# Two pairs of experts share one end, and the down weights are laid out by blocks of columns

## The chip, the cores and the metric

The kernel runs on one core of a Trainium2 chip. The metric is the device time of one execution in microseconds (us): the median of three runs of the kernel before.

## What is computed

A network of two layers works on 256 context tokens and 256 latent tokens of 1024 channels, in float32. Layer 0 has a gated linear-attention mixer (HGRN2) and then a mixture of experts over all 512 tokens; layer 1 has a latent-attention mixer (MLA) and then a mixture of experts over the 256 latent tokens, which are the output. The mixture of experts is the part that matters here. Each token goes to two of 32 experts, and an expert is

```python
def expert_block(args):
    xb, e = args
    return (jax.nn.silu(xb @ w_gate[e]) * (xb @ w_up[e])) @ w_down[e]
...
return jnp.einsum('nkd,nk->nd', y_slot.reshape(n_tok, MOE_TOP_K, d), gate_w.astype(h.dtype))
```

with `w_gate` and `w_up` of 1024 x 512 and `w_down` of 512 x 1024. The weighted sum is multiplied by a gate vector for each channel (`rG` in the kernel) and added to the residual `x`.

## The kernel before

**Pairs.** The 32 experts of a layer are worked through as 16 pairs, i = 0 to 15, in the function `stream`. Each expert has 64 slots for tokens, and a pair fills the 128 rows of the TensorE array: slots of the one expert in the left half, slots of the other in the right half, so every product of a pair is two half-wide matmuls, one for each expert's weights.

**One pair**, in the order of the program: load gate weights (two slots of 2 MB, one for each expert), `product` (L1038, 16 matmuls of 512 columns), Silu on ScalarE (L1173); load up weights, `product`; `hidden` (L1048, VectorE: Silu times up); `turn_hidden` (four transposes on TensorE, L1055, and a copy on ScalarE, L1057); `onehot` (L1062, VectorE: the matrix G that sends slots back to tokens); load down weights; `down` (L1069, two halves of 512 output columns, 16 matmuls each). Then `weighed` makes of each half two tiles yH and yL that carry the weighted result in two parts (ScalarE L1075, then VectorE L1076), and `give_back` runs once for each tile of 128 tokens (four in layer 0, two in layer 1): two matmuls with G (L1086 with yH, L1087 with yL) into one PSUM bank, a VectorE multiply by `rG` into `tmp` (L1089), and an add to `x` (L1090).

**Buffers.** yH, yL and G have one buffer each, so the next yL is written only after the last matmul that reads the one before it.

**Overlap between pairs.** `back` is a generator: the give-backs of pair i are issued in two halves during pair i+1, the first after its gate product and the second after its up product (the two `next(bk, None)`).

**The last pair** (i = 15) has nothing after it. `finish` cuts its down product into four blocks of 256 columns; block n+1 is multiplied before block n is given back. In these give-backs the odd token tiles use other PSUM banks, and the adds of the odd tiles of the first three blocks run on GpSimd (`adder=G`): six in layer 0, three in layer 1. In layer 1 each finished block is written out.

**What sets the order.** In `stream` TensorE, VectorE and ScalarE keep the order of the program (a manual schedule). All weight loads are issued by SyncE's one queue, in program order, into seven slots of 2 MB in layer 0 and nine in layer 1 that go round in a fixed list; a load waits until the slot's last reader is done. After layer 0's stream, `mla_load` loads the mixer's first weights and makes eight small matmuls (L1249), a branch on "more tokens than slots" follows (not taken with these inputs), and the mixer of layer 1 starts on all engines behind that branch.

Of the kernel before, what the change touches and what calls it, by code (L numbers as in the profile page):

```python
# [32 lines left out]
def prepare(inputs):  # L33
# [41 lines left out]
    o["rw"] = rw.reshape(2, 8, 128, 36).transpose(0, 2, 1, 3)  # L75
    o["wg"] = a["moe_w_gate"].reshape(2, 32, 128, 4096)
    o["wu"] = a["moe_w_up"].reshape(2, 32, 128, 4096)
    o["wd"] = a["moe_w_down"].reshape(2, 32, 128, 4096)
    return {k: np.ascontiguousarray(v) for k, v in o.items()}


# [1 line left out]
class K:  # L83
# [819 lines left out]
    def moe(self):  # L903
# [5 lines left out]
        with self.moe_st, ExitStack() as st:  # L909
# [108 lines left out]
                        give(xT, pt, b)  # L1018
                return xT

            def wload(src, i, parts=1, by=1, one=False):

                ws = [self.slot() for _ in range(2)]
                turns = [(c, a) for c in range(parts) for a in range(2)]
                for c, a in sorted(turns, key=lambda t: t[1]) if one else turns:
                    e = 2 * i + a
                    s_ = src[l, e] if isinstance(i, int) else src[l, bass.ds(e, 1)].rearrange("o p f -> (o p) f")
                    if parts == 1:
                        nc.sync.dma_start(ws[a], s_)
                    else:  # L1030
                        w_, s_ = [t.rearrange("p (j n c) -> p j n c", j=by, n=parts)[:, :, c, :] for t in (ws[a], s_)]
                        nc.sync.dma_start(w_, s_)
                return ws

            def product(p, xT, ws, k):
# [11 lines left out]
            def hidden(hi, p_up):  # L1047
                V.tensor_tensor(hi, hi, p_up, op=ALU.mult)  # L1048

            def turn_hidden(hi):  # L1050

                pt = self.sm()
                hv = hi.rearrange("p (q j) -> p j q", j=4)
                for j in range(4):
                    PE.transpose(pt[:, j * 128:(j + 1) * 128], hv[:, j, :], self.ident)  # L1055
                hT = hidT()
                S.copy(hT, pt.rearrange("p (j t) -> p j t", j=4))  # L1057
                return hT

# [4 lines left out]

            def down(hT, ws, n, w_):
                p = self.mm()[:, 0:w_]
                for j in range(4):
                    for a in range(2):
                        PE.matmul(p[a * 64:(a + 1) * 64, :], hT[:, j, a * 64:(a + 1) * 64],  # L1069
                                  ws[a][:, j * 1024 + n * w_:j * 1024 + n * w_ + w_], start=(j == 0), stop=(j == 3))  # L1070
                return p

            def weighed(p, wc, yH, yL):
# [4 lines left out]
            def parts():  # L1078
                return [b2.tile([128, 512], F32R, tag=t, name=t, bufs=1) for t in ("yH", "yL")]

            def give_back(tt, n, w_, Gm, yH, yL, bank=None, adder=V):

                ns = slice(n * w_, n * w_ + w_)
                pc = (bank or self.ac)()[:, 0:w_]
                g = Gm[:, tt * 128:(tt + 1) * 128]
                PE.matmul(pc, g, yH, start=True, stop=False)  # L1086
                PE.matmul(pc, g, yL, start=False, stop=True)  # L1087
                t = self.tmp()[:, 0:w_]
                V.tensor_tensor(t, pc, rG[vec(tt)][:, ns], op=ALU.mult)  # L1089
                adder.tensor_tensor(x[:, tt, ns], x[:, tt, ns], t, op=ALU.add)  # L1090

            def finish(hT, Gm, ws, wc, last):

                w_ = 256 if last else 512

                def scatter(n, yH, yL):
                    for tt in range(NT):
                        odd = last and tt % 2
                        give_back(tt, n, w_, Gm, yH, yL, self.sm if odd else None, G if odd and n < 3 else V)
                    if last and l:  # L1100
                        write_out_part(n, w_)

                yHL, todo = [], []
                for n in range(1024 // w_):
                    p = down(hT, ws, n, w_)
                    if n * w_ % 512 == 0:
                        yHL = parts()
                    yH, yL = [t[:, n * w_ % 512:n * w_ % 512 + w_] for t in yHL]
                    weighed(p, wc, yH, yL)
                    if todo:  # L1110
                        scatter(*todo.pop())
                    todo.append((n, yH, yL))
                scatter(*todo.pop())

            def pair(i, xT, fc, wc):

                pgu = []
                for src in (I["wg"], I["wu"]):
                    ws = wload(src, i)
                    p = self.mm()  # L1120
                    for k in range(8):
                        product(p, xT, ws, k)
                    pgu.append(p)
                ws = wload(I["wd"], i)
                hi = hid()
# [3 lines left out]
                finish(hT, onehot(fc), ws, wc, False)  # L1129

# [24 lines left out]
                return xT, step  # L1155

            def stream(p0, xT0):
                bk, xq, nxt, fstep = iter(()), xT0, None, None
                for i in range(16):
                    a, q = i % 2, i // 2  # L1160
                    if i and a == 0:
                        xq = nxt
                    xT = xq[a]
                    one, last = 2 if i == 1 else i == 2, i == 15
                    if i:
                        ws = wload(I["wg"], i, 4 if one else 2 if last else 1, one=one == 2 and l == 0)
                        p = self.mm()
                        for k in range(8):
                            product(p, xT, ws, k)
                    else:  # L1170
# [3 lines left out]
                    next(bk, None)  # L1174
# [10 lines left out]
                    next(bk, None)  # L1185
                    hT = turn_hidden(hi)
                    if q < 7:
                        fstep()
                    Gm = onehot(idxf[:, i:i + 1])
                    ws = wload(I["wd"], i, 4 if last or one else 1, 4 if last else 1)  # L1190
                    if last:
                        finish(hT, Gm, ws, wsl[:, i:i + 1], True)
                    else:
                        bk = back(i, [down(hT, ws, n, 512) for n in range(2)], Gm)
                        next(bk)

            def overflow():

# [334 lines left out]
```

## Time and profile before

| | |
|---|---|
| median of three runs | 1577.06 us (1576.94, 1577.06, 1578.92) |
| profiled execution | 1578.04 us |
| its span, first to last instruction | 1576.3 us |
| mean granted TensorE clock | 0.985 of full |
| TensorE busy | 1499.6 us (95%) |
| VectorE busy | 813.2 us (52%) |
| ScalarE / GpSimd busy | 449.1 / 74.9 us |
| moved by DMA | 500.80 MB, mean 318 GB/s |

The profiled execution lies 1.74 us above its own span, and 0.98 us above the median. The stream of layer 0 runs to about 919 us, the mixer of layer 1 follows, and the stream of layer 1 ends the kernel. A busy share is an average over stages with different limits, so the stages are read one by one below.

### The profile page before, as it was taken

The numbers are of one execution on the slowest core, as the hardware profiler recorded it, in microseconds if no ns is written. First come the engines' busy times: TensorE is split into PE (matmuls) and PEld (weight loads), VectorE is DVE, ScalarE is ACT, GpSimd is POOL, SyncE is SP. The second block draws the span as 40 slices with busy tenths as digits, with TensorE's granted clock in tenths as the row PEclk, the third lists the DMA queues.
The fourth block names the chain that finished last, engine by engine and source line by source line (L and its number), as shares of the span: only waits on it lengthen the run. The fifth ranks groups of instructions, "written<-read, shape, count | busy, mean of one in ns | idle before, by whom it ended". The sixth has DMA issues, their size and how long they took to land. (4 is left out here: it accounts for less than half of the span.)

```text
span 1576.3 us, 20139 instructions
## 1 busy us (share of the span) xinstructions
PE 1499.6 (95%) x8009; PEld 825.2 (52%) x8010; DVE 813.2 (52%) x1675; ACT 449.1 (28%) x938; POOL 74.9 (5%) x101
## 2 busy tenths in 40 slices
PE   7999999999899999999999999989799999998997
PEld 4777787778644544544544454447444443433433
DVE  5776647775824544544544567674534332332333
ACT  4554445553411111111111145554411111111110
POOL 0000000001300000000000011310100000000000
PEclk9999999999799999999999999999899999999999
DMA  9454534414769999999999957344799999999997
GB/s 384 165 201 177 196 136 161 188 54 161 276 240 399 429 428 426 428 427 426 427 429 423 356 218 305 141 187 142 272 392 428 427 427 428 428 427 428 427 425 268
DMA packets 63127, 500.80 MB, mean 318 GB/s; under 512 B 7024, under 2 KB 16624, under 8 KB 32816
## 3 DMA queue, kind: packets, MB, share of 16 engines
q1 hardware_dynamic: 59296, 490.87, 76.5%
q10 hardware_dynamic: 2816, 7.26, 1.4%
q0 software_dynamic: 912, 1.27, 0.3%
q8 instruction: 67, 1.10, 0.3%
q14 instruction: 36, 0.29, 0.0%
HBM read 498.26 MB, written 1.11 MB: 317 GB/s over the span
## 5 line engine op out<-in xcount | busy, mean ns | idle before, releaser
L1038 PE MATMUL mm<-w,xT 128*64 128x512 f32 x2048 | 469.9, 595 | 19.8 <-DMA w<-in_wg_dram 16.4
L1038 PEld LDWEIGHTS mm<-w,xT 128*64 128x64 f32 x2048 | 146.8, 137 | 310.7 <-issue 266.3
L1089 DVE TENSOR_TENSOR tmp<-p,rG 128x512 f32<-128x512 f32 (+1 forms) x106 | 68.0, 644 | 132.7 <-PE p L1087 132.6
L1090 DVE TENSOR_TENSOR x<-x,tmp 128x512 f32<-128x512 f32 (+1 forms) x195 | 132.4, 679 | 6.7
L1089 DVE TENSOR_TENSOR tmp<-p,x 128x512 f32<-128x512 f32 (+1 forms) x68 | 44.4, 655 | 165.1 <-PE p L1087 165.1
L1069 PE MATMUL mm<-w,x 128*64 128x512 f32 (+1 forms) x544 | 116.3, 570 | 1.6 <-ACT x L1057 1.4
L1069 PE MATMUL mm<-w,hT 128*64 128x512 f32 (+1 forms) x544 | 113.9, 570 | 1.4 <-ACT hT L1057 1.4
L889 PE MATMUL p<-sel,h2H 128*128 128x256 f32 x384 | 101.8, 300 | 1.8 <-DVE sel L879 1.8
L513 PE MATMUL mm<-hH,wH 128*128 128x512 f32 x256 | 101.9, 398 | 0.3 <-ACT wH L262 0.3
L515 PE MATMUL mm<-hH,wL 128*128 128x512 f32 x256 | 101.3, 396 | 0.5 <-DVE wL L264 0.5
L514 PE MATMUL mm<-hL,wH 128*128 128x512 f32 x256 | 100.6, 393 | 0.0
L890 PE MATMUL p<-sel,h2L 128*128 128x256 f32 x384 | 98.5, 290 | 0.0
L1076 DVE SCALAR_TENSOR_TENSOR yL<-mm,wsl,yH 128x512 fp32r<-128x512 f32 (+1 forms) x68 | 48.7, 716 | 71.6 <-ACT yH L1075 71.6
L1075 ACT ACTIVATE yH<-mm,wsl 128x512 fp32r<-128x512 f32 (+1 forms) x68 | 45.1, 663 | 123.3 <-PE mm L1069 93.2
L889 PEld LDWEIGHTS p<-sel,h2H 128*128 128x128 f32 x384 | 76.7, 200 | 5.1 <-issue 2.4
L264 DVE TENSOR_TENSOR wL<-w,wH 128x1024 fp32r<-128x1024 f32 x55 | 67.0, 1221 | 23.5 <-ACT wH L262 22.0
L1086 PE MATMUL p<-yH,G 128*128 128x512 f32 (+1 forms) x174 | 76.2, 441 | 0.9 <-DVE tmp L1089 0.9
L890 PEld LDWEIGHTS p<-sel,h2L 128*128 128x128 f32 x384 | 76.3, 199 | 1.4 <-issue 0.8
L1069 PEld LDWEIGHTS mm<-w,x 128*64 128x64 f32 x544 | 45.6, 137 | 60.0 <-issue 45.6
L262 ACT CAST wH<-w 128x1024 fp32r<-128x1024 f32 x55 | 57.3, 1047 | 63.3 <-PE mm L514 32.8
L1069 PEld LDWEIGHTS mm<-w,hT 128*64 128x64 f32 x544 | 37.5, 137 | 65.8 <-issue 59.7
L1086 PEld LDWEIGHTS p<-yH,G 128*128 128x128 f32 x174 | 32.5, 187 | 65.8 <-issue 51.5
(392 smaller groups left out, 2119.2 us busy)
## 6 DMA issues: line engine op xcount, KB each, us to landing
w<-in_wg_dram SPq DMA_DIRECT2D x52, 2048.0 KB, 18.1
w<-in_wu_dram SPq DMA_DIRECT2D x52, 2048.0 KB, 21.4
w<-in_wd_dram SPq DMA_DIRECT2D x52, 2048.0 KB, 20.2
aw<-in_ada_w_dram SPq DMA_DIRECT2D x32, 1024.0 KB, 6.0
w<-in_wd_dram SPq DMA_DIRECT2D x48, 512.0 KB, 8.7
w<-in_hg_w_dram SPq DMA_DIRECT2D x8, 2048.0 KB, 7.9
w<-in_wg_dram SPq DMA_DIRECT2D x32, 512.0 KB, 7.8
w<-in_wu_dram SPq DMA_DIRECT2D x32, 512.0 KB, 9.5
```

What stands on the lines that cost most here:

```text
L262: nc.scalar.copy(H, raw)
L264: nc.vector.tensor_tensor(L, raw, H, op=ALU.subtract)
L513: PE.matmul(p, H[:, c], hH[:, k, :], start=(k == 0), stop=False)
L514: PE.matmul(p, H[:, c], hL[:, k, :], start=False, stop=False)
L515: PE.matmul(p, L[:, c], hH[:, k, :], start=False, stop=(k == 7))
L889: self.nc.tensor.matmul(o, self.h2H[:, tt, c], r, start=(tt == 0 and k == 0), stop=False)
L890: self.nc.tensor.matmul(o, self.h2L[:, tt, c], r, start=False, stop=(last and k == 1))
L1038: PE.matmul(p[a * 64:(a + 1) * 64, :], xT[:, k, a * 64:(a + 1) * 64], ws[a][:, k * 512:(k + 1) * 512], start=(k == 0), stop=(k == 7))
L1069: PE.matmul(p[a * 64:(a + 1) * 64, :], hT[:, j, a * 64:(a + 1) * 64], ws[a][:, j * 1024 + n * w_:j * 1024 + n * w_ + w_], start=(j == 0), ...
L1086: PE.matmul(pc, g, yH, start=True, stop=False)
L1089: V.tensor_tensor(t, pc, rG[vec(tt)][:, ns], op=ALU.mult)
L1090: adder.tensor_tensor(x[:, tt, ns], x[:, tt, ns], t, op=ALU.add)
```

## The change

The host now lays the down weights of an expert out in four blocks of 256 output columns; within a block the four chunks of the contraction follow each other. A load of one block is 4 KB in a row in each partition, where it was four runs of 1 KB. `down` with 512 columns reads its moving operand as two runs of 256 columns, 1024 elements apart. This holds for every pair.

In each layer the last two pairs, 14 and 15, share one end. Pair 14's down product is no longer made before pair 15's gate product: gate and up of both pairs come first, then the down blocks of 14 and of 15, each block multiplied before the one ahead of it is given back. Layer 1 has eight blocks of 256 columns; layer 0 has two of 512 for pair 14 and four of 256 for pair 15. The give-backs of pair 14 therefore no longer run under pair 15's gate and up. The GpSimd adds are gone (all adds on VectorE), and odd token tiles always use the other banks in `finish`. Pair 15's gate and up weights are loaded ahead of pair 14's down weights.

```diff
-    o["wd"] = a["moe_w_down"].reshape(2, 32, 128, 4096)
+    wd = a["moe_w_down"].reshape(2, 32, 128, 4, 4, 256)
+    o["wd"] = wd.transpose(0, 1, 2, 4, 3, 5).reshape(2, 32, 128, 4096)
...
-                    if parts == 1:
-                        nc.sync.dma_start(ws[a], s_)
-                    else:
-                        w_, s_ = [t.rearrange("p (j n c) -> p j n c", j=by, n=parts)[:, :, c, :] for t in (ws[a], s_)]
-                        nc.sync.dma_start(w_, s_)
+                    f = slice(c * 4096 // parts, (c + 1) * 4096 // parts)
+                    nc.sync.dma_start(ws[a][:, f], s_[:, f])
...
             def down(hT, ws, n, w_):
                 p = self.mm()[:, 0:w_]
+                m = w_ // 256
                 for j in range(4):
                     for a in range(2):
-                        PE.matmul(p[a * 64:(a + 1) * 64, :], hT[:, j, a * 64:(a + 1) * 64],
-                                  ws[a][:, j * 1024 + n * w_:j * 1024 + n * w_ + w_], start=(j == 0), stop=(j == 3))
+                        w = ws[a].rearrange("p (n j c) -> p j n c", n=4, j=4)[:, j, n * m:(n + 1) * m, :]
+                        PE.matmul(p[a * 64:(a + 1) * 64, :].rearrange("p (n c) -> p n c", n=m), hT[:, j, a * 64:(a + 1) * 64], w,
+                                  start=(j == 0), stop=(j == 3))
...
-                adder.tensor_tensor(x[:, tt, ns], x[:, tt, ns], t, op=ALU.add)
...
+                V.tensor_tensor(x[:, tt, ns], x[:, tt, ns], t, op=ALU.add)
+
+            def finish(*todo, last=False):
+
+                yHL, wait = [], []
+
+                def scatter(n, w_, Gm, yH, yL, out):
                     for tt in range(NT):
-                        odd = last and tt % 2
-                        give_back(tt, n, w_, Gm, yH, yL, self.sm if odd else None, G if odd and n < 3 else V)
-                    if last and l:
+                        give_back(tt, n, w_, Gm, yH, yL, self.sm if tt % 2 else None)
+                    if out:
                         write_out_part(n, w_)
...
+                for z, (hT, i, fc, ws, w_) in enumerate(todo):
+                    for n in range(1024 // w_):
+                        p = down(hT, ws, n, w_)
+                        if n * w_ % 512 == 0:
+                            yHL = parts()
+                        yH, yL = [t[:, n * w_ % 512:n * w_ % 512 + w_] for t in yHL]
+                        weighed(p, i, yH, yL)
+                        if wait:
+                            scatter(*wait.pop())
+                        if n == 0:
+                            Gm = onehot(fc)
+                        wait.append((n, w_, Gm, yH, yL, last and l and z == len(todo) - 1))
+                scatter(*wait.pop())
...
-                    Gm = onehot(idxf[:, i:i + 1])
-                    ws = wload(I["wd"], i, 4 if last or one else 1, 4 if last else 1)
-                    if last:
-                        finish(hT, Gm, ws, wsl[:, i:i + 1], True)
-                    else:
+                    if i < 14:
+                        Gm = onehot(idxf[:, i:i + 1])
+                        ws = wload(I["wd"], i, 4 if one else 1)
                         bk = back(i, [down(hT, ws, n, 512) for n in range(2)], Gm)
                         next(bk)
+                    else:
+                        ends.append((hT, i))
+                todo = []
+                for hT, i in ends:
+                    w_ = 512 if l == 0 and i == 14 else 256
+                    todo.append((hT, wsl[:, i:i + 1], idxf[:, i:i + 1], wload(I["wd"], i, 1024 // w_), w_))
+                finish(*todo, last=True)
```

**TensorE at the end of layer 0, behind pair 14's transposes.** The numbers behind p and w are those of PSUM banks and weight slots. Before, its down matmuls (L1069) come next:

```order
L1086 MATMUL p_6437<-yH,G 128x512
L1087 MATMUL p_6437<-yL,G 128x512
L1055 MATMUL p_6443<-ident,tmp 128x128 x4
L1069 MATMUL mm<-w_3936,hT 64x512
L1069 MATMUL mm<-w_3937,hT 64x512
```

In the change pair 15's gate matmuls (L1036 there, L1038 before) stand at that place:

```order
L1086 MATMUL p_6437<-yH,G 128x512
L1087 MATMUL p_6437<-yL,G 128x512
L1053 MATMUL p_6443<-ident,tmp 128x128 x4
L1036 MATMUL mm<-w_3936,xT 64x512
L1036 MATMUL mm<-w_3937,xT 64x512
```

Pair 14's down product has moved behind gate and up of pair 15.

**VectorE at the end of layer 0.** Before, the first half of pair 14 is given back ahead of pair 15's `hidden` (L1048); these are the last of its rows, with the second half's first behind it:

```order
L1089 TENSOR_TENSOR tmp<-p_6517,rG_3389 128x512
L1090 TENSOR_TENSOR x<-x,tmp 128x512
L1076 SCALAR_TENSOR_TENSOR yL<-mm,wsl,yH 128x512
L1048 TENSOR_TENSOR tmp<-tmp,mm 128x512
L1089 TENSOR_TENSOR tmp<-p_6549,rG_3387 128x512
L1090 TENSOR_TENSOR x<-x,tmp 128x512
```

In the change `hidden` of pair 15 (L1046 there) comes ahead of all of them, and the two yL and the one G of pair 14 follow:

```order
L1046 TENSOR_TENSOR tmp<-tmp,mm 128x512
L1252 MEMSET w_3356 128x256
L1253 COPY w_3356<-colB_87 128x8x2
L1076 SCALAR_TENSOR_TENSOR yL<-mm,wsl,yH 128x512
L1060 TENSOR_SCALAR G<-iota,idxf 128x512
L1076 SCALAR_TENSOR_TENSOR yL<-mm,wsl,yH 128x512
L1089 TENSOR_TENSOR tmp<-p_6542,rG_3387 128x512
L1090 TENSOR_TENSOR x<-x,tmp 128x512
```

All eight multiplies and adds of pair 14 have moved behind pair 15's `hidden`, and the second yL ahead of the first multiply.

**VectorE a little later**, in the change alone: where the rows of pair 14 end and those of pair 15 begin.

```order
L1089 TENSOR_TENSOR tmp<-p_6597,rG_3389 128x512
L1090 TENSOR_TENSOR x<-x,tmp 128x512
L1060 TENSOR_SCALAR G<-iota,idxf 128x512
L1076 SCALAR_TENSOR_TENSOR yL<-mm,wsl,yH 128x256
L1089 TENSOR_TENSOR tmp<-p_6616,rG_3387 128x256
L1090 TENSOR_TENSOR x<-x,tmp 128x256
```

Pair 15's G stands behind the last add of pair 14; before, it stood ahead of pair 15's first block.

## Rows read from the trace of the kernel before

**Rows 1.** Busy time by window, two in each stream and the mixer of layer 1.

```profile
core 0: us, PE busy (x) PEld busy (x) DVE busy (x) ACT busy (x) POOL busy (x), PEclk, DMA share, GB/s
480.00:850.00 370.00, 370.00 (x1861) 175.50 (x1861) 179.67 (x287) 41.26 (x76) 0.00 (x0) 1.00 1.01 425
...
1108.00:1112.00 4.00, 0.00 (x0) 0.00 (x0) 4.00 (x15) 2.49 (x7) 2.69 (x2) 0.68 0.93 297
1112.00:1116.00 4.00, 2.61 (x16) 2.56 (x17) 3.91 (x14) 2.96 (x4) 2.46 (x2) 0.50 0.88 331
```

**Rows 2.** Waits from 480 to 850 us: total, times, longest.

```profile
PEld mm L1038 <- DMA w<-in_wg_dram: 0.6, 2, 0.3
```

**Rows 3.** TensorE's timeline, end of layer 0: start, us, instruction [idle <-releaser].

```profile
874.41 7.09 PE L1069 MATMUL mm<-w,hT 128*64 128x512 f32 x32 [0.68 <-ACT hT L1057]
881.33 7.04 PE L1038 MATMUL mm<-w,xT 128*64 128x512 f32 x32
888.29 0.50 PE L1086 MATMUL p<-yH,G 128*128 128x512 f32 x1
...
890.47 7.09 PE L1038 MATMUL mm<-w,xT 128*64 128x512 f32 x32
...
899.59 0.64 PE L1055 MATMUL p<-ident,tmp 128*128 128x128 f32 x4
900.90 3.67 PE L1069 MATMUL mm<-w,hT 128*64 128x256 f32 x32 [0.68 <-ACT hT L1057]
904.50 0.38 PE L1086 MATMUL p<-yH,G 128*128 128x256 f32 x1
...
905.64 1.95 PE L1069 MATMUL mm<-w,hT 128*64 128x256 f32 x16
...
919.70 1.06 PE L1307 MATMUL p<-ident,x 128*128 128x128 f32 x8 [1.56 <-DVEq L1200]
```

**Rows 4.** VectorE's timeline at the same place.

```profile
889.07 0.69 DVE L1089 TENSOR_TENSOR tmp<-p,rG 128x512 f32<-128x512 f32 x1
...
890.40 0.68 DVE L1089 TENSOR_TENSOR tmp<-p,rG 128x512 f32<-128x512 f32 x1
...
897.61 0.69 DVE L1048 TENSOR_TENSOR tmp<-tmp,mm 128x512 f32<-128x512 f32 x1 [2.48 <-PE mm L1038]
...
916.15 0.41 DVE L1089 TENSOR_TENSOR tmp<-p,rG 128x256 f32<-128x256 f32 x1
...
916.94 0.42 DVE L1089 TENSOR_TENSOR tmp<-p,rG 128x256 f32<-128x256 f32 x1
...
918.20 0.42 DVE L1090 TENSOR_TENSOR x<-x,tmp 128x256 f32<-128x256 f32 x1
```

**Rows 5.** VectorE by kind, 858 to 905 us: busy, mean ns | idle before.

```profile
L1076 DVE SCALAR_TENSOR_TENSOR yL<-mm,wsl,yH 128x512 fp32r<-128x512 f32 x3 | 2.2, 746 | 1.3 <-ACT yH L1075 1.3
...
L1062 DVE TENSOR_SCALAR G<-iota,idxf 128x512 fp32r<-128x512 f32 x2 | 1.0, 480 | 0.0
L1076 DVE SCALAR_TENSOR_TENSOR yL<-mm,wsl,yH 128x256 fp32r<-128x256 f32 x1 | 0.5, 477 | 0.0
```

**Rows 6.** ScalarE by kind, 860 to 905 us.

```profile
L1075 ACT ACTIVATE yH<-mm,wsl 128x512 fp32r<-128x512 f32 x3 | 2.1, 687 | 6.4 <-PE mm L1069 3.8 <-PE p L1086 2.6
```

**Rows 7.** The loads of the modulation weights (L208), 900 to 990 us.

```profile
DMA to landing us min/median/max: 4.8/9.1/13.9
```

**Rows 8.** The chain that ended last, its end: start, us, what.

```profile
1531.81 19.86 DMA w<-in_wu_dram
...
1561.98 1.88 PE mm L1069 x16
...
1564.53 1.93 PE mm L1069 x16
1566.48 0.48 ACT yH L1075
...
1570.04 0.42 DVE x L1090
```

More of the change, by code (lines that the diff above doesn't have):

```diff
@@ L1019, in dispatch, with wload @@
                 return xT
-            def wload(src, i, parts=1, by=1, one=False):
+            def wload(src, i, parts=1, one=False):
                 ws = [self.slot() for _ in range(2)]
@@ L1048, in hidden, with turn_hidden @@
                 V.tensor_tensor(hi, hi, p_up, op=ALU.mult)
-            def turn_hidden(hi):
+            def turn_hidden(hi, hT=None):
                 pt = self.sm()
@@ L1055, in turn_hidden @@
                     PE.transpose(pt[:, j * 128:(j + 1) * 128], hv[:, j, :], self.ident)
-                hT = hidT()
+                hT = hidT() if hT is None else hT
                 S.copy(hT, pt.rearrange("p (j t) -> p j t", j=4))
@@ L1079, in parts, with give_back @@
                 return [b2.tile([128, 512], F32R, tag=t, name=t, bufs=1) for t in ("yH", "yL")]
-            def give_back(tt, n, w_, Gm, yH, yL, bank=None, adder=V):
+            def give_back(tt, n, w_, Gm, yH, yL, bank=None):
                 ns = slice(n * w_, n * w_ + w_)
@@ L1089, in give_back @@
                 V.tensor_tensor(t, pc, rG[vec(tt)][:, ns], op=ALU.mult)
-                adder.tensor_tensor(x[:, tt, ns], x[:, tt, ns], t, op=ALU.add)
-            def finish(hT, Gm, ws, wc, last):
-                w_ = 256 if last else 512
-                def scatter(n, yH, yL):
+                V.tensor_tensor(x[:, tt, ns], x[:, tt, ns], t, op=ALU.add)
+            def finish(*todo, last=False):
+                yHL, wait = [], []
+                def scatter(n, w_, Gm, yH, yL, out):
                     for tt in range(NT):
-                        odd = last and tt % 2
-                        give_back(tt, n, w_, Gm, yH, yL, self.sm if odd else None, G if odd and n < 3 else V)
-                    if last and l:
+                        give_back(tt, n, w_, Gm, yH, yL, self.sm if tt % 2 else None)
+                    if out:
                         write_out_part(n, w_)
[L1103 to L1113, printed above, removed]
+                for z, (hT, i, fc, ws, w_) in enumerate(todo):
[11 more added lines that the diff above has]
+                scatter(*wait.pop())
             def pair(i, xT, fc, wc):
@@ L1128, in pair @@
                 hT = turn_hidden(hi)
-                finish(hT, onehot(fc), ws, wc, False)
+                finish((hT, wc, fc, ws, 512))
             def back(i, ps, Gm):
@@ L1157, in stream @@
             def stream(p0, xT0):
-                bk, xq, nxt, fstep = iter(()), xT0, None, None
+                bk, xq, nxt, fstep, ends = iter(()), xT0, None, None, []
                 for i in range(16):
@@ L1173, in stream @@
                     S.activation(hi, p, AF.Silu)
-                    next(bk, None)
+                    if not last:
+                        next(bk, None)
                     if a == 0 and q < 7:
@@ L1184, in stream @@
                     hidden(hi, p)
-                    next(bk, None)
-                    hT = turn_hidden(hi)
+                    if not last:
+                        next(bk, None)
+                    hT = turn_hidden(hi, b2.tile([128, 4, 128], F32, tag="xT", name="hT2", bufs=3) if last else None)
                     if q < 7:
                         fstep()
-                    Gm = onehot(idxf[:, i:i + 1])
-                    ws = wload(I["wd"], i, 4 if last or one else 1, 4 if last else 1)
-                    if last:
-                        finish(hT, Gm, ws, wsl[:, i:i + 1], True)
-                    else:
+                    if i < 14:
+                        Gm = onehot(idxf[:, i:i + 1])
+                        ws = wload(I["wd"], i, 4 if one else 1)
                         bk = back(i, [down(hT, ws, n, 512) for n in range(2)], Gm)
                         next(bk)
+                    else:
[5 more added lines that the diff above has]
+                finish(*todo, last=True)
             def overflow():
```

## The prediction

> **What bounds the kernel now.** I read the busy time by windows first, then the waits inside the long stage, then the timelines of the two places that the change touches, and last the chain that ended last. In layer 0's stream TensorE is busy in all of 370 us at full clock, VectorE in half of that [rows 1], and the loads cost it 0.6 us in total [rows 2]: this stage is TensorE's, and what a pair does on VectorE is free there as long as it runs under the next pair's products. At its end this changes. The reader is to see that pair 14's give-backs stand right behind a product (888.29 behind the gate product that began at 881.33) and that the next product starts at 890.47 without waiting for VectorE [rows 3]; VectorE needs 1.33 us for each 512-wide multiply and add (889.07 to 890.40) [rows 4] and has 7 us of product to do it in. Only the four blocks of pair 15 are uncovered: the last add ends at 918.62 (918.20 + 0.42) [rows 4], and TensorE starts the mixer of layer 1 at 919.70 after 1.56 us of waiting for the branch, which follows that add [rows 3]. So VectorE's last add of layer 0 sets when layer 1 begins. The end of layer 1 is different: the chain runs through the load of pair 15's up weights, which lands at 1551.67 (1531.81 + 19.86), and from there through TensorE to the last add [rows 8].
>
> **Layer 0's end, step by step**, on the time axis of before. Pair 14's transposes end at 873.73 (874.41 less its wait of 0.68) [rows 3]. Gate and up of pair 15 now follow at once, 6.96 us each (881.33 to 888.29): 887.65. Then `hidden`, 0.69 [rows 4], and the four transposes, 0.64 [rows 3]: 889.0. The order shows that pair 14's down does not wait for pair 15's ScalarE copy, so one wait of 0.68 before pair 14's down and one before pair 15's are saved, and about 0.7 for `hidden` comes in. Pair 14's two blocks A0 and A1 take 6.92 (874.41 to 881.33): 895.9. The give-backs of A0 take 2.18 on TensorE (888.29 to 890.47): 898.1.
>
> Here VectorE falls behind. There is one yL, so A1's yH and yL wait for the last matmul of A0's give-backs (before, yH already waits for that matmul, 2.6 us in three [rows 6]), and in program order the second yL stands ahead of A0's first multiply. Queued behind it are all eight multiplies and adds of pair 14, and the PSUM banks that A1's give-backs need. yH 0.69 [rows 6], yL 0.75 [rows 5]: A0's multiplies start at 899.5. Four times 1.33 is 5.3: 904.8. A1's give-backs end at about 904.6, since their banks come free with these multiplies; pair 15's first block B0 then gets yH and yL, 0.48 each [rows 5, 8]: 905.6. A1's multiplies and adds: 910.9. Only then come pair 15's G, 0.48, and the second yL, 0.48 [rows 5]: 911.9. B0's four multiplies and adds at 0.79 (916.15 to 916.94) [rows 4]: 915.0. TensorE meanwhile, from the G at 911.4: give-backs of B0 1.14 (904.50 to 905.64), block B2 1.9, give-backs of B1 1.14 [rows 3]: 915.6; yH and yL of B2: 916.5. B1: 919.7, yL of B3: 920.2, B2 and B3: 926.5. Consecutive VectorE instructions overlap a little (0.69 and 0.69 start 1.33 apart, not 1.38 [rows 4]), which over the 20 rows that I took in full is worth some 0.6: 925.9 against 918.62. **+7.3**, with +6 (the four short waits between yH, yL and TensorE all vanish) and +8.5 as bounds. The six adds taken from GpSimd are in this sum: all 16 multiplies count 0.79 with their add.
>
> **The clock.** TensorE has nothing to do from 906.5 (A1's give-backs end at 904.6, B1's 1.9 behind them) until G at 911.4, 4.9 us. A stretch of 4 us in which TensorE did nothing shows a granted clock of 0.68, and the next 4 us 0.50, the lower of its levels (1.2 GHz) [rows 1]. If the clock falls here too, B0's and B1's give-backs and B2, 4.15 us, take up to 8.3, and yL of B2 is late by as much: 0 to +4.2. That stretch lay in a longer wait than this one, and its 0.68 says that the fall came inside it, so I take half: **+2.0**. The Trainium skill ("TensorE: Matmul & The Clock Gate", the part on the HAM clock gate) says that the throttled state is the default and that activity releases it, and warns of waits that throttle the array again in every round. By that rule the fall is to be expected, and the sum would be nearer +4 than 0; the rows above show the fall only for the longer wait.
>
> **The start of the mixer.** TensorE stands still again behind the last give-backs (about 924 to 927.5), so the mixer may begin at the lower clock. The order also puts four matmuls with modulation weights early in the mixer; their load is issued behind the branch, and such loads take 4.8 us at least, 9.1 typically [rows 7], about what the mixer has until then. Bounds 0 and +3; before, the wait ahead of the mixer was short and the loads were not what TensorE waited for at 919.70 [rows 3], so I take a value near the lower end, **+0.5**. From there the mixer is a serial chain and layer 1's weights wait for the slots that it frees: the delay goes through in full.
>
> **Layer 1's end.** Pair 15's up weights no longer queue behind pair 14's down weights. Two slots are 4.19 MB, at 425 GB/s [rows 1] 9.87 us: the up weights land at 1541.8. Half a product (3.5), `hidden` and transposes: 1546.6. Then eight blocks: two in 3.67, the other six each 2.55 after the one before (1561.98 to 1564.53) [rows 3, 8]: 1565.6. VectorE needs 0.48 + 2 x 0.79 = 2.1 for a block there and keeps up, but pair 15's G stands behind pair 14's last add here too: about 1.1. 1566.7 against 1566.46 (1564.53 + 1.93) [rows 8]; the last adds, free of GpSimd, give some 0.3 back. **0**, with +1 above. Below it is -3.1: the last down weights can land no earlier than 1561.5 (1541.8 + 2 x 9.87), and a block of 1.9 ends 1563.4 then.
>
> **The layout.** The loads of down weights in longer runs are not waited for in layer 0 [rows 2] and not in the chain at the end [rows 8]: 0, covered by products as long as the loads lead. The 512-wide `down` now reads its moving operand in two runs, 480 times in layer 0. No row shows that. The nearest are the transposes: four with an operand read at a stride of four elements take 0.64, eight with an even one 1.06 [rows 3]. By the mean of each that is 0.03 more per instruction, 14 us for 480; but the difference of the two, 0.105 for each further one, leaves 0.22 for the start of a group, and the strided four fit that with no excess. I take 0.
>
> **Sum.** +7.3 +2.0 +0.5 +0 = +9.8 on the profiled execution, 1576.3 + 1.74 + 9.8 = 1587.8. That execution lies 0.98 above the median, so the median becomes 1577.06 + 9.8 = **1586.9**.
>
> **Rivals.**
> The clock holds: the sum without its term, with up to 0.5 at the mixer, 1584.4 to 1584.9. For it: the wait is shorter than the one in which it fell. Chance 0.20.
> VectorE keeps up, and it ends on the faster side: pair 14's give-backs hide under the down matmuls of pair 15 as they hid under gate and up. It decides at the point where VectorE's 5.3 + 0.75 per 512-wide block stay under TensorE's 3.46 + 2.18. They are 6.1 against 5.6, and in the 256-wide blocks 0.48 + 3.2 against 1.9 + 1.14, so it does not; if it did, layer 0 would end about 1 earlier by the saved copies and layer 1 up to 3.1 earlier: about 1574.5. Chance 0.05.
> The delay of layer 0 is taken up behind it, because layer 1's stream is limited by its loads and not by when its first product starts: then only what delays the loads counts, and the time is 1577 to 1580. Against it: the slots that these loads need are the mixer's. Chance 0.07.
> The two runs slow `down`: every 0.01 us per matmul costs 4.8 in layer 0, so 1592 and more. Chance 0.08.
> My forecast keeps 0.60. The range of 1581 to 1592 takes in the first rival, the bounds of the clock and of the mixer's start, and leaves out the others. Within 0.2% (3.2 us, about what a measurement of this kernel can tell from no change) lies the third rival, 0.07; faster is the second, 0.05; slower the rest, 0.88.
>
> **What the profile after would show.** On the axis of before, gate and up of pair 15 without a wait behind the transposes; VectorE busy without a gap of more than 1 us from about 899 to 926; TensorE idle some 5 us ahead of the first 256-wide give-back, with a VectorE row as releaser, and a granted clock under 1 there if the second term is right; the mixer's first transposes near 928.5; in layer 1 the whole of the stream later by the same amount, up to pair 15's up product, and the end as far from it as the sum says. I am wrong if VectorE has gaps in that stretch, if the 32 down matmuls of an early pair last longer than 6.92, or if layer 1's first weight loads are not later by as much as layer 0's last add.

## The result and the profile after

The changed kernel takes 1590.23 us in the median of five runs (1588.63 to 1591.40), the kernel before 1577.06 in five (1571.60 to 1578.92): a ratio of 1.009 with a 95% interval of 1.0072 to 1.0107, so slower by 13.2 us. The forecast was 1586.9. The profiled execution took 1590.23 us with a span of 1588.5.

The end of layer 0, first TensorE's timeline of the changed kernel (start, us, instruction, in brackets the idle time ahead of it and what ended it):

```profile
872.46 13.96 PE L1036 MATMUL mm<-w,xT 128*64 128x512 f32 x64
887.28 0.75 PE L1053 MATMUL p<-ident,tmp 128*128 128x128 f32 x4 [0.86 <-DVE tmp L1046]
887.96 7.09 PE L1069 MATMUL mm<-w,hT 128*64 128x512 f32 x32
894.98 0.50 PE L1086 MATMUL p<-yH,G 128*128 128x512 f32 x1
...
903.66 1.95 PE L1069 MATMUL mm<-w,hT 128*64 128x256 f32 x16
910.38 0.55 PE L1086 MATMUL p<-yH,G 128*128 128x256 f32 x1 [4.77 <-DVE G L1060]
...
912.35 3.68 PE L1069 MATMUL mm<-w,hT 128*64 128x256 f32 x16
...
929.32 1.47 PE L1315 MATMUL p<-ident,x 128*128 128x128 f32 x8 [4.01 <-PEq L1208]
...
942.46 2.97 PE L1329 MATMUL mm<-w,w 128*128 128x416 f32 x8
```

Gate and up of pair 15 run through behind the transposes, and the two waits of 0.68 that stood ahead of the down products [rows 3] are one of 0.86. Then TensorE rests 4.77 us for pair 15's G, and the block behind it takes 3.68 us where the one before it took 1.95. The windows of the same kernel show the granted clock in that place (the PEclk column) and again at the start of the mixer:

```profile
core 0: us, PE busy (x) PEld busy (x) DVE busy (x) ACT busy (x) POOL busy (x), PEclk, DMA share, GB/s
904.00:908.00 4.00, 1.61 (x16) 0.79 (x12) 3.85 (x7) 0.48 (x2) 0.00 (x0) 1.00 0.01 2
908.00:912.00 4.00, 1.62 (x7) 1.65 (x8) 3.38 (x8) 0.00 (x0) 0.00 (x0) 0.67 0.00 0
912.00:916.00 4.00, 4.00 (x19) 1.89 (x18) 2.78 (x9) 0.00 (x0) 0.00 (x0) 0.50 0.01 4
916.00:920.00 4.00, 4.00 (x30) 2.56 (x28) 2.23 (x6) 0.95 (x2) 0.00 (x0) 0.98 0.00 0
...
928.00:932.00 4.00, 2.68 (x13) 2.42 (x14) 1.12 (x7) 2.56 (x5) 1.08 (x4) 0.73 0.41 145
```

VectorE's timeline, the same kernel and place:

```profile
897.62 0.75 DVE L1076 SCALAR_TENSOR_TENSOR yL<-mm,wsl,yH 128x512 fp32r<-128x512 f32 x1 [4.03 <-ACT yH L1075]
898.28 0.68 DVE L1089 TENSOR_TENSOR tmp<-p,rG 128x512 f32<-128x512 f32 x1
...
904.45 0.68 DVE L1089 TENSOR_TENSOR tmp<-p,rG 128x512 f32<-128x512 f32 x1
...
909.75 0.48 DVE L1060 TENSOR_SCALAR G<-iota,idxf 128x512 fp32r<-128x512 f32 x1
...
911.18 0.42 DVE L1089 TENSOR_TENSOR tmp<-p,rG 128x256 f32<-128x256 f32 x1 [0.55 <-PE p L1087]
...
917.70 0.48 DVE L1076 SCALAR_TENSOR_TENSOR yL<-mm,wsl,yH 128x256 fp32r<-128x256 f32 x1 [2.74 <-ACT yH L1075]
...
927.68 0.42 DVE L1090 TENSOR_TENSOR x<-x,tmp 128x256 f32<-128x256 f32 x1
```

VectorE rests 4.03 us although A0's first give-back is in its bank from 895.7 on: the second yL stands ahead in its order and waits. From there it works with short gaps (0.55 us at most) until 928.1, but for 2.74 us ahead of the yL of B2. Most of that gap is the slow stretch of TensorE: in keep_busy5 below, at full clock, it is 0.87.

The end of layer 1, TensorE's timeline of the changed kernel (PEld is the loading of its weights): pair 15's G is waited for there too, and so are, for 0.79 us in the middle of their product, the up weights of pair 15.

```profile
1542.08 14.93 PE L1036 MATMUL mm<-w,xT 128*64 128x512 f32 x64
...
1553.36 0.20 PEld L1036 LDWEIGHTS mm<-w,xT 128*64 128x64 f32 x4 [0.79 <-DMA w<-in_wu_dram]
...
1558.54 3.67 PE L1069 MATMUL mm<-w,x 128*64 128x256 f32 x32
...
1573.42 0.35 PE L1086 MATMUL p<-yH,G 128*128 128x256 f32 x1 [1.03 <-DVE G L1060]
```

The start of layer 0's stream moves by some us from one execution to the next (pair 14's transposes begin at 873.10 before, 871.90 after, and between 868.77 and 873.52 in the kernels below). So the places are compared by their distance from the start of those transposes: the end of layer 0's last add, the first transposes of the mixer, the transposes of the same early pair of layer 1 (1189.32 before), and the end of the kernel's last add. All in us, each from one profiled execution:

| | layer 0's last add | mixer starts | early pair, layer 1 | last add ends |
|---|---|---|---|---|
| before | 45.52 | 46.60 | 316.22 | 697.36 |
| the change | 56.20 | 57.42 | 328.97 | 710.90 |
| layout_alone | 45.51 | 46.59 | 316.55 | 697.95 |
| l1_alone | 45.51 | 46.61 | 315.03 | 696.39 |
| l0_alone | 55.08 | 56.40 | 327.89 | 708.26 |
| early_g | 52.44 | 53.42 | 323.53 | 704.46 |
| keep_busy | 65.89 | 66.84 | 336.98 | 719.26 |
| keep_busy5 | 53.52 | 54.74 | 324.25 | 705.98 |
| busy_tail | 53.98 | 62.40 | 331.47 | 711.83 |
| two_y | 49.96 | 50.93 | 321.82 | 702.06 |
| before_no_gpsimd | 46.62 | 47.83 | 317.09 | 699.35 |
| before_two_y | 44.56 | 46.04 | 314.57 | 696.33 |
| best | 44.58 | 46.22 | 314.89 | 696.52 |

Of the change's +13.5 by this measure, 10.7 are there at layer 0's last add, 1.9 come between the mixer's start and layer 1's early pairs (271.55 against 269.62), and 0.8 at layer 1's end (381.93 against 381.14). One profile each tells the last two badly: three kernels that end layer 0 as before (before, layout_alone, l1_alone) take 268.4 to 270.0 from the mixer's start to the early pair.

### The profile page after: what moved, and what is told of

It is laid out like the page before. It is cut to its first block, busy times and chain, and to the rows that moved or that the text cites. A ratio compares the mean times of both kernels' runs of the same rounds, so it can differ in the third digit from the quotient of the medians.

```text
span 1588.5 us, 20248 instructions
## 1 busy us (share of the span) xinstructions
PE 1506.6 (95%) x8049; PEld 831.7 (52%) x8050; DVE 817.3 (51%) x1694; ACT 449.6 (28%) x940; POOL 68.6 (4%) x92
## 5 line engine op out<-in xcount | busy, mean ns | idle before, releaser
L1036 PE MATMUL mm<-w,xT 128*64 128x512 f32 x2048 | 468.9, 595 | 19.3 <-DMA w<-in_wg_dram 16.4
L1036 PEld LDWEIGHTS mm<-w,xT 128*64 128x64 f32 x2048 | 148.4, 137 | 307.6 <-issue 262.9
L1069 PE MATMUL mm<-w,hT 128*64 128x512 f32 (+1 forms) x608 | 123.6, 558 | 0.0
L1069 PE MATMUL mm<-w,x 128*64 128x512 f32 (+1 forms) x512 | 108.7, 569 | 0.4 <-DMA w<-in_wd_dram 0.4
L1069 PEld LDWEIGHTS mm<-w,hT 128*64 128x64 f32 x608 | 42.3, 139 | 67.8 <-issue 61.4
L1069 PEld LDWEIGHTS mm<-w,x 128*64 128x64 f32 x512 | 43.5, 137 | 54.2 <-issue 40.0
```

Of the source, the lines that this page charges most:

```text
L1036: PE.matmul(p[a * 64:(a + 1) * 64, :], xT[:, k, a * 64:(a + 1) * 64], ws[a][:, k * 512:(k + 1) * 512], start=(k == 0), stop=(k == 7))
L1069: PE.matmul(p[a * 64:(a + 1) * 64, :].rearrange("p (n c) -> p n c", n=m), hT[:, j, a * 64:(a + 1) * 64], w, start=(j == 0), stop=(j == 3))
```

## The experiments

**layout_alone.** The kernel before with the first hunks of the change's diff (host layout, contiguous loads, `down`) and nothing else:

```diff
-                                  ws[a][:, j * 1024 + n * w_:j * 1024 + n * w_ + w_], start=(j == 0), stop=(j == 3))
+                        w = ws[a].rearrange("p (n j c) -> p j n c", n=4, j=4)[:, j, n * m:(n + 1) * m, :]
```

> The kernel before with the new layout of the down weights alone (loads in runs of 4 KB, the 512-wide down product reads two runs of 256 columns); the order of all instructions is as before. Theory of the joint end: no change, within 3 us of 1577, 32 down matmuls of an early pair of layer 0 still 6.9 us, layer 1's end as before. Rival, the layout costs: 0.01 us more for each of 480 matmuls in layer 0 would be +5 us, seen as 32 down matmuls of 7.2 us.

1575.53 us against 1576.34 of the kernel before, ratio 0.9996 (0.9983 to 1.0008). The layout costs nothing that can be measured. The changed kernel's groups of instructions by line from 490 to 860 us agree; its down matmuls (L1069) read two runs and have the same mean as the product's, which read one. The kernel before, whose down matmuls read one run, shows the second line word for word:

```profile
L1036 PE MATMUL mm<-w,xT 128*64 128x512 f32 x798 | 176.1, 594 | 0.0
L1069 PE MATMUL mm<-w,hT 128*64 128x512 f32 x416 | 92.1, 595 | 0.0
```

**l1_alone and l0_alone.** The joint end in one layer, the other ending as before with its GpSimd adds:

```diff
+            solo = l in (0,)
...
-                    if not last:
+                    if solo or not last:
                         next(bk, None)
...
-                    if i < 14:
+                    if i < 14 or solo and i == 14:
```

(with `(1,)` in l0_alone).

> The change with the joint end in layer 1 only; layer 0 ends as before, GpSimd adds included. Theory: nearly all of the rise goes, the last add of layer 0 stands 45 us behind pair 14's transposes as before (55.6 with the change), and what is left is layer 1's end, about +0.7 us: 1577 to 1579. Rival, the rise comes from the mixer or from layer 1's own end: 1585 and more.

1577.12 against 1576.34, ratio 1.0006 (0.9995 to 1.0017).

> The change with the joint end in layer 0 only; layer 1 ends as before, GpSimd adds included. Theory: the rise stays, less layer 1's 0.7 us: 1588 to 1590, with the last add of layer 0 55.6 us behind pair 14's transposes. Rival (layer 1's end): 1580 or less.

1587.97, ratio 1.0078 (1.0064 to 1.0092). The rise is layer 0's end and what follows from it. The 0.7 us for layer 1's end are below what these runs resolve.

The end of layer 0 in l0_alone is the same program as in the change, and its last add stands at 55.08 where the change has 56.20 (the 55.6 and 45 of the two expectations count from the end of pair 14's transposes). The lines of l0_alone show where the 1.1 us went: the same wait of 4.77 and a fall of the clock behind it, but block B2 takes 2.73 and not 3.68, and the clock is back at 1.00 in the window from 912 us.

```profile
908.50 0.45 PE L1086 MATMUL p<-yH,G 128*128 128x256 f32 x1 [4.77 <-DVE G L1060]
...
910.38 2.73 PE L1069 MATMUL mm<-w,hT 128*64 128x256 f32 x16
```

```profile
908.00:912.00 4.00, 3.50 (x16) 2.69 (x18) 3.44 (x9) 0.00 (x0) 0.00 (x0) 0.57 0.00 0
```

So what the fall costs differs by 1.1 us between two executions of the same instructions.

**early_g.** Pair 15's G in a buffer of its own, made behind pair 14's:

```diff
+                Gm = (b2.tile([128, NTOK], F32R, tag="xT", name="G2", bufs=3) if own else
+                      b2.tile([128, NTOK], F32R, tag="G", name="G", bufs=1))
...
-                            Gm = onehot(fc)
+                            if z == 0:
+                                Gs = [onehot(t[2], own=y > 0) for y, t in enumerate(todo)]
+                            Gm = Gs[z]
```

> The change with pair 15's G in a buffer of its own, made right behind pair 14's G instead of behind pair 14's last add. Theory: TensorE's wait of 4.8 us ahead of the first 256-wide give-back shrinks to what the yL and the free banks ask for, and so the clock does not fall there: in layer 0 the 2.9 us that the fall cost and some 0.5 us of G go, in layer 1 about 0.7 us of the wait of 1.03; in all 3 to 4.5 us less than the change, 1586 to 1587.5. VectorE's eight 512-wide multiplies and adds and the wait for the one yL stay, so it stays 9 or more above before. Rival, VectorE alone sets the end and the wait of TensorE costs nothing: within 1 us of the change.

1585.22 us, ratio 1.0061 (1.0046 to 1.0077), 5 us under the change and a little under the expected 1586. At layer 0's last add it is 3.8 earlier (3.4 expected), and the wait of 4.77 is gone. The windows of early_g show full clock there, and the clock still falls at the start of the mixer:

```profile
908.00:912.00 4.00, 3.18 (x24) 2.01 (x24) 3.86 (x10) 0.00 (x0) 0.00 (x0) 1.00 0.01 4
...
924.00:928.00 4.00, 3.00 (x13) 2.75 (x13) 0.88 (x6) 2.52 (x5) 1.09 (x4) 0.51 0.56 178
```

**keep_busy and keep_busy5.** The clock by itself: matmuls into a bank that nobody reads fill TensorE's wait and make nothing else earlier.

```diff
+                        if last and l == 0 and z == 1 and n == 1:
+                            pd = self.mm()
+                            for k in range(20):
+                                PE.matmul(pd, hT[:, 0, :], ws[0][:, 0:512], start=True, stop=True)
```

> The change, plus 20 matmuls of 512 columns in layer 0 behind pair 15's second down block, into a bank that nobody reads: they fill TensorE's wait for pair 15's G (4.8 us) without making anything else earlier. Theory of the clock: the granted clock stays at 1.00 through that place, the four blocks behind it are not stretched, and layer 0's last add stands 2.5 to 3.3 us nearer to pair 14's transposes than with the change (56.2): about 53.3. Rival, the clock costs nothing because VectorE sets the end: 56 as with the change.

1600.83 us, ratio 1.0156 (1.0141 to 1.0172): the filler was mis-sized, and the last add stands at 65.89. I had taken the x32 in 7.09 us [rows 3] for 32 half-wide matmuls. They are the records of 16: by the code a product makes eight matmuls for each expert (and a half of `down` four, eight in all and not the 16 given above), and the trace holds two records of each. A half-wide one thus takes 0.44 us, and a full-wide one of the filler twice that, 0.87 (17.43 us for 20, in 40 records, TensorE's timeline of keep_busy):

```profile
905.13 17.43 PE L1108 MATMUL mm<-w,hT 128*128 128x512 f32 x40
922.01 0.68 PE L1086 MATMUL p<-yH,G 128*128 128x256 f32 x1
```

So the same with `range(5)`:

> keep_busy with 5 filler matmuls in place of 20: in keep_busy each 128 x 128 by 512 matmul took 0.85 us, so 20 of them lasted 17 us and not the 4.3 that were meant; 5 last 4.3 and end before pair 15's G is there. Theory of the clock: granted clock 1.00 through layer 0's end, give-backs of B0, block B2 and give-backs of B1 take 4.3 us together (6.8 in the change), the last add of layer 0 at 53 to 54 us behind the start of pair 14's transposes (56.2 in the change), total 2 to 3 us under the change. Rival, the clock costs nothing there: 56 us.

Layer 0's last add stands at 53.52, 2.7 under the change, inside the expected 53 to 54. TensorE's timeline of keep_busy5, the yL of B2 on VectorE, and the windows:

```profile
902.41 4.56 PE L1108 MATMUL mm<-w,hT 128*128 128x512 f32 x10
907.24 0.36 PE L1086 MATMUL p<-yH,G 128*128 128x256 f32 x1 [0.28 <-DVE G L1060]
...
908.36 1.95 PE L1069 MATMUL mm<-w,hT 128*64 128x256 f32 x16
...
911.89 0.48 DVE L1076 SCALAR_TENSOR_TENSOR yL<-mm,wsl,yH 128x256 fp32r<-128x256 f32 x1 [0.87 <-ACT yH L1075]
```

```profile
904.00:908.00 4.00, 3.72 (x13) 1.74 (x12) 3.67 (x8) 0.00 (x0) 0.00 (x0) 1.00 0.00 0
908.00:912.00 4.00, 4.00 (x34) 2.77 (x34) 3.00 (x9) 0.47 (x1) 0.00 (x0) 1.00 0.01 4
...
920.00:924.00 4.00, 0.49 (x3) 0.52 (x4) 2.41 (x8) 0.81 (x1) 0.44 (x3) 0.92 0.06 12
924.00:928.00 4.00, 4.00 (x17) 3.27 (x15) 1.41 (x5) 3.19 (x9) 0.64 (x1) 0.65 0.92 345
```

The G still comes last, but the clock holds at 1.00 and block B2 takes 1.95 where it took 3.68. The total, 1588.20 with a ratio of 1.0074 (1.0058 to 1.0090), is 2 under the change's 1590.23, though with intervals that overlap; the last add is what shows the cause. Against the 55.08 of l0_alone the last add is 1.6 earlier, against the 56.20 of the change 2.7: that is the range of what the clock costs here.

**busy_tail.** early_g with 14 such matmuls, in the program behind layer 0's last give-backs:

```diff
                 self.mla_load()
+                pd = self.mm()
+                for k in range(14):
+                    PE.matmul(pd, self.ident, self.iota[:, 0:512], start=True, stop=True)
```

> early_g, plus 14 matmuls of 512 columns behind the last give-backs of layer 0, into a bank that nobody reads, so that TensorE comes to the mixer of layer 1 without the 3.8 us of rest that it had in early_g (where the mixer's first eight transposes took 1.94 us and the granted clock was 0.51 in their stretch). Theory, the mixer starts slowly because of that rest: clock 1.00 there, eight transposes in 1.06, the first of the mixer's 416-column groups of eight 1.5 to 2.5 us nearer to the mixer's start than in early_g (13.8), and up to as much from the total. Rival, the mixer is later because four matmuls with modulation weights (two microseconds) now stand early in it: the group stays 12.8 or more behind the mixer's start.

1592.50 us, ratio 1.0099 (1.0084 to 1.0115): the same mis-sizing makes the mixer start late (62.4 us behind the transposes), so the total says nothing. The pace from there does. TensorE's timeline of busy_tail at the mixer's start, then that of early_g, then the matching line of the kernel before (its mixer starts at 919.70 [rows 3]):

```profile
935.74 1.06 PE L1321 MATMUL p<-ident,x 128*128 128x128 f32 x8 [0.45 <-DVE bsel L1273]
...
947.47 2.97 PE L1335 MATMUL mm<-w,w 128*128 128x416 f32 x8
```

```profile
925.00 1.94 PE L1318 MATMUL p<-ident,x 128*128 128x128 f32 x8 [3.79 <-DVEq L1211]
...
938.80 2.97 PE L1332 MATMUL mm<-w,w 128*128 128x416 f32 x8
```

```profile
930.48 2.97 PE L1321 MATMUL mm<-w,w 128*128 128x416 f32 x8
```

With no rest ahead of it the mixer reaches its first group of 416 columns in 11.73 us, with the rest in 13.80 (13.14 in the change); before it took 10.78 (919.70 to 930.48), with the modulation matmuls later in its order. So both theories hold a part: 2.1 for the clock and 1.0 for the order. Some of it is given back: from the mixer's start to layer 1's early pair busy_tail takes 269.07, early_g 270.11.

busy_tail shows one thing more. Up to the last give-backs its program is that of early_g, and yet the clock fell in its joint end, without any long wait: the longest of TensorE's in the 10 us ahead was 0.59.

```profile
904.44 0.79 PE L1087 MATMUL p<-yH,G 128*128 128x512 f32 x1 [0.59 <-DVE tmp L1090]
...
905.59 3.01 PE L1070 MATMUL mm<-w,hT 128*64 128x256 f32 x16
```

```profile
904.00:908.00 4.00, 3.56 (x14) 1.90 (x16) 3.26 (x6) 0.47 (x1) 0.00 (x0) 0.57 0.01 2
```

So the full clock of early_g is what one execution showed, not what making G early secures. The fall cost VectorE 0.3 us here (its wait ahead of the yL of B0 is 0.67 and not 0.37); the rest of the 1.5 by which the last add is later than in early_g comes from filler matmuls that ran between the last give-backs.

**two_y.** early_g with a second buffer for yH and yL, in turn with the first:

```diff
-                            yHL = parts()
+                            if last and turn % 2:
+                                Y2 = Y2 or b2.tile([128, 1024], F32R, tag="xT", name="Y2", bufs=3)
+                                yHL = [Y2[:, 0:512], Y2[:, 512:1024]]
+                            else:
+                                yHL = parts()
+                            turn += 1
```

> early_g, plus a second buffer for yH and yL in the joint ends, in turn with the first. Theory: the second yL no longer waits for the first give-backs, VectorE's multiplies begin with the first bank that TensorE fills (about 24.5 us behind the start of pair 14's transposes instead of 26.4), and the small waits ahead of the later yL go: layer 0's last add at 49.5 to 50.5 us (early_g 52.4), total 2 to 3 us under early_g. From there VectorE's sum of work alone is left, 4 to 5 us more than before. Rival, the banks or TensorE set the pace: within 1 us of early_g.

1582.73, ratio 1.0032 (1.0020 to 1.0043). VectorE's first multiply stands 24.6 us behind the transposes (26.4 in early_g), the last add 2.5 earlier at 49.96. VectorE's timeline of two_y at that place:

```profile
897.43 0.75 DVE L1077 SCALAR_TENSOR_TENSOR Y<-mm,wsl,Y 128x512 fp32r<-128x512 f32 x1 [1.83 <-ACT Y L1076]
898.10 0.68 DVE L1090 TENSOR_TENSOR tmp<-p,rG 128x512 f32<-128x512 f32 x1
```

With no wait of VectorE over 0.34 us from there to its last add, 4.4 us more than before remain. The clock fell here too, with no wait of TensorE above 0.82 in the 10 us ahead, and block B2 took 3.56 (TensorE's timeline and the window of two_y); VectorE had work enough in hand not to wait for it.

```profile
908.51 0.39 PE L1087 MATMUL p<-yH,G 128*128 128x256 f32 x1 [0.82 <-DVE tmp L1090]
...
908.96 3.56 PE L1070 MATMUL mm<-w,hT 128*64 128x256 f32 x16
```

```profile
908.00:912.00 4.00, 3.49 (x16) 2.01 (x18) 3.86 (x10) 0.00 (x0) 0.00 (x0) 0.61 0.00 0
```

**before_no_gpsimd.** The kernel before with `adder` left at VectorE:

```diff
-                        give_back(tt, n, w_, Gm, yH, yL, self.sm if odd else None, G if odd and n < 3 else V)
+                        give_back(tt, n, w_, Gm, yH, yL, self.sm if odd else None)
```

> The kernel before with the nine GpSimd adds on VectorE and nothing else. It prices that part of the change alone: six adds of 0.38 us come to VectorE in layer 0's end (+2.3) and the four or five adds that lasted 0.72 beside GpSimd go back to 0.42 (-1.5), so the last add of layer 0 about 1 us later, 46 to 47 us behind the start of pair 14's transposes (45.5 before), total within 2 us of before. Rival, the GpSimd adds carried the end and their loss is a main part of the rise: 49 us or more.

The last add comes 1.1 us later, as expected. The total, 1581.14 with a ratio of 1.0032 (1.0018 to 1.0046), is 4.4 above the kernel before, where at most 2 were expected, and wide (1575.2 to 1585.6; the runs of the kernel before beside them 1571.5 to 1579.9). The profiled execution was one of the short ones (1575.71) because it reached pair 14's transposes 4.2 us earlier than the kernel before (868.86 against 873.10); from there to the last add it takes 2.0 more (699.35 against 697.36). Where the rest of the 4.4 lies is not shown. What the profile does show is TensorE at rest ahead of the mixer for 4.19 us (1.56 before [rows 3]), at the lower clock behind it:

```profile
916.69 1.94 PE L1307 MATMUL p<-ident,x 128*128 128x128 f32 x8 [4.19 <-PEq L1200]
```

```profile
916.00:920.00 4.00, 3.21 (x13) 2.83 (x14) 1.18 (x6) 3.58 (x7) 1.07 (x4) 0.57 0.61 217
```

Its first group of 416 columns starts at 930.32, 13.63 behind the mixer's start (10.78 before), as late as in the kernels with a joint end. So in this execution the adds on VectorE alone brought the long rest ahead of the mixer and the slow start behind it.

**before_two_y and best.** The second buffer alone in the kernel before (this edit); and the versions that did best put together, layer 0 as in l1_alone, layer 1 as in two_y, the second buffer in both.

```diff
-                    if n * w_ % 512 == 0:
+                    if last and n == 2:
+                        Y2 = b2.tile([128, 1024], F32R, tag="xT", name="Y2", bufs=3)
+                        yHL = [Y2[:, 0:512], Y2[:, 512:1024]]
+                    elif n * w_ % 512 == 0:
```

> The kernel before with a second buffer of yH and yL for the last two blocks of pair 15, nothing else. Theory: before, the third yH waits 3.56 us for the first buffer and VectorE 1.0 for it; that wait goes and layer 0's last add comes 0.5 to 1 us earlier, layer 1's end 0 to 0.5: 1575.5 to 1576.5. Rival: VectorE's sum of work sets the end, no difference.

1575.38 against 1576.85, ratio 0.9995 (0.9985 to 1.0006): layer 0's last add is 1.0 earlier, the total not clear of noise.

> Layer 0 ends as before (pair 14 given back under pair 15's products, odd adds on GpSimd), layer 1 with the joint end, pair 15's G made early, and a second buffer of yH and yL in both. Theory: layer 0's last add at 44.5 to 45.5 us (45.5 before), layer 1's part from its first pairs to its end 1 us shorter than before (two_y 380.2 against 381.1): 1574.5 to 1576.5, 1 to 2 us under before. Rival, layer 1's end is set by its loads and products alone: no difference from before.

1574.86, ratio 0.9986 (0.9973 to 0.9999), the lowest median here: 2.0 under the kernel before, at the edge of noise, and 0.5 under before_two_y, inside it. The shorter end of layer 1 that was expected (380.2) is not there: from the early pair to the last add it takes 381.63, before 381.14. Its profiled execution and that of before_two_y differ by 0.2 us at the last add (696.52 and 696.33), so there is no sign that the joint end in layer 1 adds anything to the buffer.

## Why the prediction was right, term by term

**Layer 0's end without the clock: +7.3 forecast, 8.0 measured** (keep_busy5 against before). By the order of the runs the change's 10.7 us divide into 2.7 for the clock (the change to keep_busy5; 1.6 from l0_alone), 1.1 for making G earlier (keep_busy5 to early_g), 2.5 for the one buffer of yH and yL (early_g to two_y) and 4.4 that stay (two_y to before). Each is a difference of two profiled executions. That the 4.4 are VectorE's work that no product covers any more is argued from two_y, where VectorE hardly waits, and not tested by itself; before_no_gpsimd prices the adds taken from GpSimd at 1.1 in the old end, and it was not tried how much they are in the joint one. The steps of the forecast were met within 0.6 us: first multiply of A0 25.8 us behind the transposes' end (forecast 25.8), of A1 32.0 (31.9), of B0 38.7 (38.2).

**The clock: +2.0 forecast, 1.6 to 2.7 measured.** The mechanism was right: the clock fell in the wait for G, and with the wait filled it did not (keep_busy5). The size was taken from the middle of two ends, and that it came so near is partly luck: give-backs, block and give-backs that take 4.2 us at full clock took 6.8 in the change (910.38 to 917.20), where the clock stayed at 0.50 through all of 912 to 916 us, and 5.7 in l0_alone (908.50 to 914.19). The Trainium skill ("TensorE: Matmul & The Clock Gate", the part on the HAM clock gate) says that the default state is throttled and that activity releases the throttle. That keep_busy5 kept the clock by useless work agrees. What the prediction did not see is that the length of the wait is not all: in busy_tail and two_y the clock fell in the same place with waits of 0.82 at most.

**The start of the mixer: +0.5 forecast; 2.5 measured at its first group of 416 columns, about 2 at layer 1's early pair.** This is the term that was mis-sized most. I chose a value near the lower end because TensorE's wait ahead of the mixer had been short before; but the forecast itself had TensorE at rest from 924 to 927.5, and the rest measured 4.01 us. The clock fell to 0.73, and the order of the matmuls with modulation weights took another part: 0.1 us came up to the mixer's start, and from there the first group of 416 columns came at 13.14 instead of 10.78. before_no_gpsimd has the same rest and the same late group without any joint end, so this term does not need the joint end. How much of it stays to the end is not settled: from the mixer's start to the early pair of layer 1 the kernels with a rest of 3.7 us or more take 269.3 to 271.6, those without 268.4 to 270.0.

**Layer 1's end: 0 forecast, +0.8 measured** in one profile (381.93 against 381.14), inside its bounds and not resolved by l1_alone. The path was as forecast: the up weights land 9.9 us earlier in layer 1's stream (352.5 behind the early pair, before 362.4), are still waited for inside their product, and G costs 1.03.

**The layout: 0 forecast, 0 measured.** The working gave no reason for it: the 0.105 and the 0.22 were taken from the very groups of four and eight that they were to test, so the four had to fit. The 480 are records, of 240 matmuls. It was layout_alone that showed the 0.

**The signs.** One sign of being wrong came true: VectorE has a gap, of 2.74 us, in the stretch where it was to have none above 1. The forecast did not agree with itself there, since its clock term makes the yL of B2 late; without the fall the gap is 0.87 (keep_busy5). The others did not: the 32 records of an early pair's down product still take 6.92 (1177.81 to 1184.73), and layer 1's first weight load starts 12.7 us later by distance from the transposes (1016.94 before, 1028.47 after), more than the 10.7 of layer 0's last add. The mixer's first transposes stand at 930.5 on the axis of before (forecast 928.5).

**The rivals.** "The clock holds" fell with the windows, "VectorE keeps up" and "the delay is taken up" with the table, "the two runs slow `down`" with layout_alone. The sum of the terms by the profiles is 13.5, by the medians 13.2, where 9.8 were forecast: in the change's own profile no term came out below its forecast, so the errors added up.

## What to carry to other kernels

Work of a slower engine that lies under another engine's products is free only there: before moving products ahead of it, add up what that engine has left to do at the end, here eight multiplies and adds of 1.33 us. Then read that engine's order for what stands ahead of its first ready instruction, since a one-hot matrix of 0.48 us and a second yL in the wrong place cost 1.1 and 2.5 us here. And price a wait of TensorE twice, by its length and by the clock behind it (1.6 to 2.7 us here), and do so from more than one execution.

## What was not expected of the hardware

Each of the nine rests of TensorE of 3.75 to 4.77 us, in the joint end and ahead of the mixer, was followed by a stretch of 4 us at a lower granted clock (0.50 to 0.73). In most of those ahead of the mixer its eight transposes took 1.94 us, in the change 1.47, in keep_busy still 1.06, with the fall just behind them (0.62 from 940 to 944 us). Rests of 1.56 to 1.94 us there left the eight at 1.06. But a rest of that length was not needed: the clock fell to 0.61 in two_y and 0.57 in busy_tail while TensorE had been partly busy, with no wait above 0.82 us, and held at 1.00 in early_g with waits like these. Why it did so in one execution and not in the other is open.

One 128 x 128 matmul of 512 float32 columns took 0.87 us (20 in 17.43), as much as two of the half-wide ones (16 in 7.09).

And taking nine adds from GpSimd, 1.1 us by the last add of layer 0, made the median 4.4 us longer; why the longer of those runs were longer is open, since only a short one was profiled.
